# The FFN down projection as seven products per pair of column tiles

## The chip, the core and the metric

The kernel runs on one core of a Trainium2 chip. A core has five engines with a queue each, which run their instructions in order: TensorE (PE: matmuls, with weight loads shown apart as PEld), VectorE (DVE), ScalarE (ACT), GpSimd (POOL) and SyncE (SP, which here only starts DMAs). Matmul results land in PSUM, which has 8 banks of 128 partitions x 512 f32; everything else lives in SBUF. DVE and ACT read PSUM, POOL doesn't. Engines wait for one another by semaphores that a framework sets from what each instruction reads and writes; the order on each engine is the order in which the program emits the instructions (a manual schedule). The metric is device time in microseconds (us), the median of several runs.

## What is computed

One layer of a diffusion backbone for 1024 latent tokens (after 256 context tokens) of width D = 1024: an S5 mixer, a SwiGLU feed-forward network (FFN) of hidden width 2816, and a final norm. The change is in the FFN alone:

```
def swiglu(h, w1, w3, w2):
    return (jax.nn.silu(h @ w1) * (h @ w3)) @ w2
...
x = x + m_l[5][:, None] * swiglu(h_l, ffn_w1[i], ffn_w3[i], ffn_w2[i])
...
return rms_norm(x, norm_final)
```

`h @ w1` and `h @ w3` are the up projection, the product with `w2` the down projection, `m_l[5]` a gate per output channel.

## The kernel before, in words

**The tiles.** The hidden width is cut into NFT = 22 column tiles of 128 ("ft"). For each, the up projection makes 128 x 1024 values g (hidden channel x token), and the down projection multiplies them by 128 rows of `w2` and adds the result to the residual `Y`, which stays in SBUF for all 1024 tokens (8 blocks `s` of 128 tokens, 8 blocks `k` of 128 channels).

**Each product is three matmuls.** An f32 value x is split into hi (x rounded to the narrower matmul type, an ACT cast) and lo (x - hi, a subtraction), and a product is hi·hi + hi·lo + lo·hi (`mm3`, lines 1259 to 1261). `mm4` makes one such product over 512 input channels: 12 matmuls of 128x128 by 128x512. All element-wise work between two tensors goes through the helper `tt` (line 70), so nearly all of it stands on line 70 in the profile and is told apart by the names of its tiles.

**The up projection** of tiles 2 to 21 uses seven products in place of eight (a 2x2 block scheme of Strassen's kind over channel halves, token halves and the two weights): `up` (line 1379) calls `mm(ft, j)` for j = 0 to 6. Their weight operands come from `raw`, four 512-wide pieces of w1 and w3, loaded by `raw13` (SP, line 1172): POOL forms sums and differences (`s5`, `raw[:, 2]`, `raw[:, 0]`, `raw[:, 1]`), and `op_split` puts hi (ACT, line 1201) and lo (POOL) into one of four slots of a ring, `ring`. The moving operands `BV[j]` are made beforehand (`t3_steps`, `t24_steps`, `t1_steps`); `t1_go` finishes the last of them during tile 2. The products' results (`pu`, one PSUM bank each, four banks in turn) are combined by DVE in `t0` to `t3`, with two Silu's on ACT; `gate_up` splits g into hi (ACT, line 1270) and lo (DVE).

**The down projection** (`down`) goes over 8 token blocks and 2 channel halves; each of these 16 makes 3 matmuls into a bank `pd` (four in turn), and DVE adds it to `Y`, 512 elements at a time. `load2` multiplies the 128 x 1024 tile of `w2` by the gate (DVE, 1024 elements) and splits it (ACT line 1002, POOL); `raw2` (SP) loads the next one into the same buffer.

**The order.** After the warm-up tiles 0 and 1, for tile ft = 2 to 19: `load2(ft)`, `up(ft)`, which emits product 0 of ft+1 before its last DVE work, then `down([ft])` with the POOL work of `prep(ft + 1)` between its steps. Tiles 20 and 21 have one `down` in common, in which also the final norm and the stores are made. One tile is 84 + 48 = 132 matmuls.

The kernel before, in the profile's names: `pu` and `pd` are PSUM tiles, `ru`, `rxa`, `rxc`, `r`, `ra`, `c` SBUF regions (`rxc` holds `raw`, `c` the ring, the split g and `w2`, `ru` the residual `Y`, the raw `w2` and `t0`, `t1`; `rxa` holds `t2`, `t3`).

Of the kernel before, what the change touches and what calls it, by code (L numbers as in the profile page):

```python
# [10 lines left out]
F32 = mybir.dt.float32  # L11
R32 = mybir.dt.float32r
I32 = mybir.dt.int32
AF = mybir.ActivationFunctionType
# [3 lines left out]
P = 128  # L18
D = 1024
# [3 lines left out]
NFT = FH // P  # L23
# [14 lines left out]
def s5_ffn_kernel(tc, a, out):  # L38
    nc = tc.nc
    V, S, E, PE, SY = nc.vector, nc.scalar, nc.gpsimd, nc.tensor, nc.sync  # L40
    ctx = ExitStack()
    with ctx:
        ctx.enter_context(tc.manual_schedule())
        sb = ctx.enter_context(tc.tile_pool(name="sb", bufs=1))
        def region(tag, kb, dt=F32):
            return sb.tile([P, int(kb * 256)], dt, tag=tag, name=tag)

        def view(reg, kb, shape, parts=P):
            off = int(round(kb * 256))
# [12 lines left out]
        RXa, RXc = region("rxa", 8), region("rxc", 8)  # L62

        def bc(ap, axis, n):
            sh = list(ap.shape)
# [3 lines left out]
        def tt(o, x, y, op, eng=V):  # L69
            eng.tensor_tensor(out=o, in0=x, in1=y, op=op)  # L70
# [10 lines left out]
        MUL, ADD, SUB = OP.mult, OP.add, OP.subtract  # L81
# [33 lines left out]
        U = view(RU, 0, [G, 160])  # L115
        Y = view(RU, 0, [8, T, P])
# [524 lines left out]
        MB = view(RXa, 0, [2, D])  # L641
# [397 lines left out]
        for i in range(10):  # L1039
# [18 lines left out]
            if i in WSP:  # L1058
                j = 1 - WSP.index(i)
# [111 lines left out]
        def raw13(ft, a0=0, a1=4):  # L1171
            SY.dma_start(wraw[:, 512 * a0:512 * a1], a["w13"][ft].rearrange("p w k n -> p (w k n)")[:, 512 * a0:512 * a1])
# [6 lines left out]
        for cq in range(4):  # L1179
            for s in range(4):  # L1180
                k = 4 * cq + s
# [12 lines left out]
        NPL = 2  # L1194
        CNT = (((0, 0, 0, 0), (2, 2, 2, 0)), ((3, 3, 3, 3), (3, 2, 2, 0)))
        raw = wraw.rearrange("p (a n) -> p a n", a=4)
        ring = [[view(W0, 4 * i + 2 * j, [4, P]) for j in range(2)] for i in range(4)]
        OP_ = {}

        def t_split(o, x, eng):  # L1200
            S.copy(o[0], x)  # L1201
# [44 lines left out]
        def gb(ft):  # L1246
            return GB[ft == NFT - 1]

        def raw2(ft):
            SY.dma_start(w2raw, a["w2"][ft * P:(ft + 1) * P])  # L1250

        def load2(ft):
            tt(w2raw, w2raw, MB[:, 1], MUL)
            split(w2raw, gb(ft)[2:], E)
            if ft + 1 < NFT:
                raw2(ft + 1)

        def mm3(pu, wh, wl, bh, bl, start, stop):
            PE.matmul(pu, wh, bh, start=start, stop=False)  # L1259
# [3 lines left out]
        def mm4(pu, w, b, start, stop):  # L1263
            for k in range(4):
                mm3(pu, w[0][:, k], w[1][:, k], b[0][:, :, k], b[1][:, :, k], start and k == 0, stop and k == 3)

        def gate_up(ft, n, t):
            ns = slice(512 * n, 512 * n + 512)
            gh, gl = gb(ft)[:2]
            S.copy(gh[:, ns], t)  # L1270
            tt(gl[:, ns], t, gh[:, ns].bitcast(F32), SUB)
# [87 lines left out]

        def prep(ft):  # L1360

            if ft > NPL:
                op_split(ft, 1, raw[:, 1])
                yield
# [8 lines left out]
            tt(raw[:, 1], raw[:, 1], raw[:, 0], SUB, E)  # L1373
            yield

        def mm(ft, j):
            pu = pu_()
            mm4(pu, OP_[ft, j], BV[j], True, True)
            return pu

        def up(ft, pu, at={}):

            t0, t1, t2, t3 = tmp
            more = ft + 1 < NFT

            def go(j):
                if j in at:
                    at[j]()

            S.copy(t0, pu)  # L1390
            op_split(ft, 4, raw[:, 3])
            go(0)
            if more:
                raw13(ft + 1, 0, 1)
                raw13(ft + 1, 2, 4)
            tt(t1, mm(ft, 1), t0, ADD)
            S.activation(t1, t1, AF.Silu)
            op_split(ft, 5, raw[:, 1])
            if more:
                raw13(ft + 1, 1, 2)  # L1400
            go(1)
            tt(t0, mm(ft, 2), t0, ADD)
            op_split(ft, 6, s5)
            go(2)
            tt(t2, mm(ft, 3), t0, ADD)
            go(3)
            if more:
                op_split(ft + 1, 0, raw[:, 0])
            pu = mm(ft, 4)
            nx = prep(ft + 1) if ft == NFT - 2 else iter(())  # L1410
            next(nx, None)
            next(nx, None)
            tt(t3, t2, pu, SUB)
            tt(t1, t1, t3, MUL)
            gate_up(ft, 0, t1)
            tt(t0, mm(ft, 5), t0, ADD)
            next(nx, None)
            pu = mm(ft, 6)
            tt(t0, pu, t0, ADD)
            S.activation(t0, t0, AF.Silu)  # L1420
            tt(t2, pu, t2, ADD)
            pu = mm(ft + 1, 0) if more else None
            tt(t0, t0, t2, MUL)
            gate_up(ft, 1, t0)
            for _ in nx:
                pass
            return pu

        def down(fts, last, *others):
            for s in range(T):  # L1430
                for n in range(2):
                    pd = pf([512])
# [44 lines left out]
        h2s(7, tba[1], 0)  # L1477
        h2s(7, tba[1], 1)
        raw2(0)
        rest = iter(())  # L1480
        up_plain(0, 0, rest, {2: lambda: together(h2t_steps(7, pf, tba[1], 0), h2t_steps(7, pf, tba[1], 1)), 3: lambda: mod_row(1, pf)})
        load2(0)
# [13 lines left out]
        NPU[0] = 4  # L1496
        pu = mm(NPL, 0)
        down([NPL - 1], False, prep(NPL))

        def t1_go():  # L1500
            for _ in range(3):
                next(rest, None)

        for ft in range(NPL, NFT - 1):
            load2(ft)
            pu = up(ft, pu, {j: t1_go for j in range(4)} if ft == NPL else {})
            if ft < NFT - 2:
                down([ft], False, prep(ft + 1))
        up(NFT - 1, pu, {2: lambda: load2(NFT - 1)})
# [61 lines left out]
```

## Time and profile before

| | |
|---|---|
| median of 3 runs | 1080.21 us (1078.52 to 1081.13) |
| the profiled execution: span from the first to the last instruction | 1084.0 us |
| mean granted TensorE clock in it | 0.977 |
| instructions | 16631 |
| PE busy, DVE busy, POOL busy, ACT busy | 91%, 70%, 58%, 39% |
| stretch of tiles 2 to 21 | from about 464 us to the end |

For the profiled execution only its span is given; it is 3.8 us above the median of the runs. In the profile a matmul's shown duration overlaps with the next one's, so the rate is read from starts, not from durations. "L70" in front of a row is the helper `tt`; "128x512 f32<-128x512 f32" gives output and input shape, "x" the count, then busy us and mean ns of one. In a timeline, the first number is the start, the second the duration, and in brackets stands how long the engine had been idle and who released it.

### The profile page before, as it was taken

Reading aid. Unit: us, or ns where it says so; the run is one execution under the profiler, and the core shown is the slowest. Engines: PE = TensorE matmul, PEld = TensorE weight load, DVE = VectorE, ACT = ScalarE, POOL = GpSimd, SP = SyncE. Lnnn points to the kernel's source line nnn. Section 1 sums busy time; section 2 is a strip of 40 time slices with the busy share of each in tenths; the row PEclk is TensorE's granted clock in tenths of the full one; section 3 lists DMA queues with packets and bytes.
Section 4 is the critical chain, followed back from the end, with each engine's and each line's share of the span. In section 5 each row is a group of like instructions: output and inputs, shape, how many; then the busy total and the mean of one; then the engine's idle time right before and its main releaser. Section 6 shows DMA issues by size and latency. Waiting matters only on the chain.

```text
span 1084.0 us, 16631 instructions
## 1 busy us (share of the span) xinstructions
PE 990.4 (91%) x6088; PEld 790.4 (73%) x6088; DVE 762.3 (70%) x1783; ACT 418.7 (39%) x833; POOL 631.4 (58%) x501
## 2 busy tenths in 40 slices
PE   4898795656899999999999999999999999999997
PEld 1466521345799997887888888888888888888875
DVE  8979699970665686898766666666766666666657
ACT  4477620453964565423122222222222222222236
POOL 4599666881274364966565555665555555556563
PEclk9998997987999999999999999999999999999999
DMA  8966679675333102110111111111011111111104
GB/s 310 318 124 125 187 231 312 185 142 118 104 114 116 42 2 78 59 38 21 58 59 59 59 59 59 59 59 32 31 56 59 59 59 59 60 59 59 55 23 156
DMA packets 54946, 104.60 MB, mean 96 GB/s; under 512 B 4432, under 2 KB 25168, under 8 KB 53840
## 3 DMA queue, kind: packets, MB, share of 16 engines
q1 hardware_dynamic: 46656, 85.57, 23.7%
q0 software_dynamic: 3888, 14.16, 7.0%
q10 hardware_dynamic: 4320, 3.81, 1.1%
q8 instruction: 48, 0.79, 0.3%
q14 instruction: 34, 0.28, 0.1%
HBM read 83.20 MB, written 6.16 MB: 82 GB/s over the span
## 4 chain that ended last, share of the span: by engine, by line
PE 71%; DMA 9%; POOL 6%; DVE 6%; ACT 5%; issue 2%; SPq 1%; ACTq 0%; DVEq 0%; POOLq 0%
PE pu L1261 11%; PE pu L1260 11%; PE pu L1259 11%; PE pd L1259 7%; PE pd L1260 7%; PE pd L1261 7%; PE pe L1024 3%; PE pe L1025 3%; PE pe L1023 3%; DVE ru L70 2%; POOL c L70 2%; DMA c<-in_ada_w 2%; DMA kd<-r 1%; PE pm L514 1%; DVE rxa L70 1%
## 5 line engine op out<-in xcount | busy, mean ns | idle before, releaser
L70 POOL TENSOR_TENSOR c<-rxc,c 128x512 fp32r<-128x512 f32 x128 | 167.8, 1326 | 185.1 <-ACT c L1201 180.2
L70 DVE TENSOR_TENSOR ru<-pd,ru 128x512 f32<-128x512 f32 x336 | 226.5, 690 | 0.0
L1259 PE MATMUL pu<-ra,c 128*128 128x512 f32 x432 | 168.4, 390 | 0.6 <-ACT ra L1201 0.3
L1261 PE MATMUL pu<-ra,c 128*128 128x512 f32 x432 | 168.4, 390 | 0.6 <-POOL c L70 0.6
L1260 PE MATMUL pu<-ra,c 128*128 128x512 f32 x432 | 168.2, 389 | 0.6 <-DVE ra L70 0.6
L1201 ACT CAST c<-rxc 128x512 fp32r<-128x512 f32 x128 | 76.8, 617 | 188.0 <-POOL rxc L70 107.3
L1259 PE MATMUL pd<-c 128*128 128x512 f32 x336 | 131.0, 390 | 0.7 <-DVE ru L70 0.7
L1260 PE MATMUL pd<-c 128*128 128x512 f32 x336 | 130.7, 389 | 0.0
L1261 PE MATMUL pd<-c 128*128 128x512 f32 x336 | 130.7, 389 | 0.0
L70 DVE TENSOR_TENSOR ru<-pu,ru 128x512 f32<-128x512 f32 x84 | 57.8, 688 | 83.2 <-PE pu L1261 52.4
L70 POOL TENSOR_TENSOR c<-ru,c 128x1024 fp32r<-128x1024 f32 x22 | 53.0, 2407 | 81.7 <-ACT c L1002 73.0
L1261 PEld LDWEIGHTS pu<-ra,c 128*128 128x128 f32 x432 | 81.1, 188 | 18.5 <-POOL c L70 1.7
L1259 PEld LDWEIGHTS pu<-ra,c 128*128 128x128 f32 x432 | 81.1, 188 | 18.1 <-ACT ra L1201 0.8
L1260 PEld LDWEIGHTS pu<-ra,c 128*128 128x128 f32 x432 | 81.1, 188 | 17.7 <-POOL c L70 0.9
L1259 PE MATMUL pu<-c,c 128*128 128x512 f32 x192 | 74.9, 390 | 0.0
L1261 PE MATMUL pu<-c,c 128*128 128x512 f32 x192 | 74.7, 389 | 0.0
L1260 PE MATMUL pu<-c,c 128*128 128x512 f32 x192 | 74.7, 389 | 0.0
L1259 PEld LDWEIGHTS pd<-c 128*128 128x128 f32 x336 | 63.1, 188 | 15.0 <-DVE ru L70 1.9
L1261 PEld LDWEIGHTS pd<-c 128*128 128x128 f32 x336 | 63.1, 188 | 13.2
L1260 PEld LDWEIGHTS pd<-c 128*128 128x128 f32 x336 | 63.1, 188 | 12.9
L70 POOL TENSOR_TENSOR c<-rxc,rxa 128x1024 f32<-128x1024 f32 x30 | 62.0, 2138 | 16.2 <-PE pw L655 10.4
L70 DVE TENSOR_TENSOR ru<-ru,rxa 128x512 f32<-128x512 f32 (+1 forms) x62 | 62.5, 1008 | 7.1 <-ACT ru L1420 3.1
(333 smaller groups left out, 2137.3 us busy)
## 6 DMA issues: line engine op xcount, KB each, us to landing
c<-in_ada_w SPq DMA_DIRECT2D x64, 256.0 KB, 5.4
ru<-in_w SPq DMA_DIRECT2D x22, 512.0 KB, 3.6
c<-c POOLq DMA_DIRECT2D x20, 512.0 KB, 6.7
rxc<-in_w SPq DMA_DIRECT2D x38, 256.0 KB, 4.5
rxc<-in_w SPq DMA_DIRECT2D x19, 512.0 KB, 5.1
ra<-in_ada_w SPq DMA_DIRECT2D x10, 512.0 KB, 11.9
ru<-in_xT SPq DMA_DIRECT2D x4, 1024.0 KB, 8.5
ra<-kd SPq DMA_DIRECT2D x16, 256.0 KB
```

Of the source, the lines that this page charges most:

```text
L70: eng.tensor_tensor(out=o, in0=x, in1=y, op=op)
L514: PE.matmul(pm[32 * b:32 * b + 2], sc3[:, k, 1 - h:3 - h], ada_tile(i), start=i < 4, stop=i >= 60, tile_position=(0, 32 * b))
L1023: PE.matmul(pz, h_[:, k], wH[:, k], start=n == 0, stop=False)
L1024: PE.matmul(pz, h_[:, k], wL[:, k], start=False, stop=False)
L1025: PE.matmul(pz, l_[:, k], wH[:, k], start=False, stop=n == 7)
L1201: S.copy(o[0], x)
L1259: PE.matmul(pu, wh, bh, start=start, stop=False)
L1260: PE.matmul(pu, wh, bl, start=False, stop=False)
L1261: PE.matmul(pu, wl, bh, start=False, stop=stop)
```

## The change

For the nine pairs of tiles (2, 3), (4, 5), ... (18, 19) the down projection of both tiles together is made by a second seven-product scheme, over the two tiles, the two halves of the tokens (s = 0 to 3, 4 to 7) and the two halves of the output channels. A product "D j" is 4 token blocks x 3 matmuls of 512 columns, 12 matmuls, in four PSUM banks. Tiles 0, 1, 20 and 21 keep the old way.

- **Seven products in three PSUM chains.** D1, D7, D6 and D5 add up in the four banks of `XT` (only D1 starts a new sum), D2 and D3 in the four banks of `UT`, D4 alone in `XT`. After each product the running sum is added to (or taken from) one quadrant of `Y` (`d_add(j, h)`, two DVE instructions of 128x1024 per product). For this the quadrant of the second channel half and first token half of `Y` is kept as a difference between `to_diff` (in tile 2) and `from_diff` (in tile 20), four DVE instructions of 1024 elements each.
- **`UT` is shared:** its four banks also take the up products "U j" (bank (j + 3) mod 4), which had a pool of four banks.
- **Operands of g:** DVE forms sums and differences of the four half tiles of g (`rA`, `rB`, `rC`, `t3`) and splits them into four slots `GS` (hi on ACT, lo on DVE).
- **Operands of w2:** two buffers `w2r`, loaded together; the gate is applied by DVE (`gate2`), and POOL forms four sums and differences in place.
- **One ring for all products:** the weights or `w2` operands of all U and D products go through the four slots in the order of `seq`; `produce(i + 4)` is emitted after product i's own work, and its hi cast (ACT) waits until product i, which used the slot, is done.
- **The order in a pair** (f even): U(f,0), then of the pair before D2, D6, D3, D5, then U(f,1), D4, then U(f,2) to U(f,6), D1 of this pair, U(f+1,0), D7, U(f+1,1) to U(f+1,6). That is 21 products, 252 matmuls.
- A region `rw` of 6 KB is added for the second `w2` buffer and `rC`, and the scratch that POOL's own DMAs use for descriptors is set to 8192 bytes.

```diff
-        w2raw = view(RU, 32, [D])
+        w2r = [view(RU, 32, [D]), view(RW, 0, [D])]
...
+        def gate2(ft):
+            tt(w2r[ft % 2], w2r[ft % 2], MB[:, 1], MUL)
...
+        XT = pF.tile([P, 4, 512], F32, tag="x", name="xt")
+        UT = pF.tile([P, 4, 512], F32, tag="u", name="ut")
+
+        RG = [ring[i] for i in range(4)]
+        GS = [[view(G2, 4 * i + 2 * j, [512]) for j in range(2)] for i in range(4)]
...
+        for f in list(PAIRS) + [NFT - 2]:
+            lead = [("U", f, 0), ("D", f - 2, 2), ("D", f - 2, 6), ("D", f - 2, 3), ("D", f - 2, 5), ("U", f, 1), ("D", f - 2, 4)]
+            seq += lead if f > NPL else [("U", f, 0), ("U", f, 1)]
+            seq += [("U", f, j) for j in range(2, 7)]
+            if f in PAIRS:
+                seq += [("D", f, 1), ("U", f + 1, 0), ("D", f, 7)]
+                seq += [("U", f + 1, j) for j in range(1, 7)]
+        seq += [("U", NFT - 1, j) for j in range(7)]
...
+        def produce(i):
...
+            if kind == "D":
+                x = w2_op(j)
+                (b11, b12), (b21, b22) = WB
+                if j == 6:
+                    tt(b12, b22, b11, SUB, E)
+                elif j == 4:
+                    tt(b21, b21, b12, SUB, E)
+                t_split(o, x, E)
+                if j == 1:
+                    tt(b11, b12, b11, SUB, E)
+                    tt(b12, b22, b12, SUB, E)
+                if j == 4:
+                    raw2(ft + 2)
+                    raw2(ft + 3)
+                return
+            x = (raw[:, 0], raw[:, 1], raw[:, 0], raw[:, 2], raw[:, 3], raw[:, 1], s5)[j]
+            t_split(o, x, E)
+            if j == 0:
+                tt(s5, raw[:, 2], raw[:, 3], ADD, E)
+            elif j == 1:
+                tt(raw[:, 2], raw[:, 0], raw[:, 2], SUB, E)
+                tt(raw[:, 0], s5, raw[:, 0], SUB, E)
+            elif j == 3:
+                tt(raw[:, 1], raw[:, 1], raw[:, 0], SUB, E)
...
+        def d_mm(i):
...
+            gh, gl = GS[{1: 0, 7: 1, 2: 0, 6: 1, 3: 2, 5: 3, 4: 0}[j]]
+            bank = UT if j in (2, 3) else XT
+            for s in range(4):
+                cs_ = slice(s * P, s * P + P)
+                for n, (w, b) in enumerate(((gh, wh), (gh, wl), (gl, wh))):
+                    PE.matmul(bank[:, s], w[:, cs_], b, start=j in (1, 2, 4) and n == 0, stop=n == 2,
+                              skip_group_check=j not in (1, 2, 4))
...
+            y = Y[:, k0:k0 + 4, s0 + 2 * h:s0 + 2 * h + 2].rearrange("p k s n -> p s k n")
+            tt(y, y, bank[:, 2 * h:2 * h + 2].rearrange("p s (k n) -> p s k n", k=4), op)
...
+            else:
+                tt(t0, pu, t0, ADD)
+                S.activation(t0, t0, AF.Silu)
+                tt(t2, pu, t2, ADD)
...
+                elif f:
+                    tt(rB, t0, t2, MUL)
+                    tt(rA, rA, rB, SUB)
+                else:
+                    tt(t3, t0, t2, MUL)
+                    tt(rA, t3, rA, SUB)
...
+        def after_u0(ft):
+
+            if NPL <= ft - 1 < NFT - 2 and ft % 2 == 0:
+                hi(GS[1], rA)
+                tt(rC, rA, rC, SUB)
+                lo(GS[1], rA)
+                hi(GS[2], rC)
+
+        def post_d(j):
+
+            if j == 1:
+                hi(GS[1], rA)
+                d_add(1, 0)
+                lo(GS[1], rA)
+                d_add(1, 1)
+            elif j == 2:
+                d_add(2, 0)
+                lo(GS[2], rC)
+                d_add(2, 1)
+                tt(rB, rB, t3, ADD)
+                hi(GS[3], rB)
+            elif j == 6:
+                d_add(6, 0)
+                lo(GS[3], rB)
+                d_add(6, 1)
+            elif j == 3:
+                hi(GS[0], t3)
+                d_add(3, 0)
+                d_add(3, 1)
+                lo(GS[0], t3)
+            else:
+                d_add(j, 0)
+                d_add(j, 1)
...
+        for i, (kind, ft, j) in enumerate(seq):
+            if i:
+                (u_mm if kind == "U" else d_mm)(i)
+            if kind == "D":
+                post_d(j)
+            else:
+                post_u(ft, j)
+                if j == 0:
+                    after_u0(ft)
+            if kind == "U" and ft in PAIRS and j in (2, 3):
+                gate2(ft + j - 2)
+            produce(i + 4)
+            if kind == "U":
+                if ft == NPL and j < 4:
+                    t1_go()
+                if ft == NPL and j == 5:
+                    to_diff()
+                if ft == NFT - 2 and j in (2, 3):
+                    from_diff(j - 2)
```

More of the change, by code (lines that the diff above doesn't have):

```diff
@@ L1373, in prep, with pd_ @@
             tt(raw[:, 1], raw[:, 1], raw[:, 0], SUB, E)
+            raw13(ft + 1, 0, 1)
             yield
[L1376 to L1427, printed above, removed]
+        def pd_(i):
+            return XT[:, i % 4] if XT is not None else pf([512])
+        XT = None
         def down(fts, last, *others):
@@ L1479, in s5_ffn_kernel @@
         raw2(0)
+        raw2(1)
         rest = iter(())
@@ L1495, in s5_ffn_kernel @@
         pF = psF.__enter__()
-        NPU[0] = 4
-        pu = mm(NPL, 0)
-        down([NPL - 1], False, prep(NPL))
+        XT = pF.tile([P, 4, 512], F32, tag="x", name="xt")
+        UT = pF.tile([P, 4, 512], F32, tag="u", name="ut")
+        RG = [ring[i] for i in range(4)]
+        GS = [[view(G2, 4 * i + 2 * j, [512]) for j in range(2)] for i in range(4)]
+        rA, rB, rC = R0[:, 0:512], R0[:, 1036:1548], view(RW, 4, [512])
+        t0, t1, t2, t3 = tmp
+        WB = [[w[:, 512 * n:512 * n + 512] for n in range(2)] for w in w2r]
@@ new lines, in w2_op @@
+        def w2_op(i):
+            (b11, b12), (b21, b22) = WB
+            return {1: b11, 7: b12, 2: b21, 6: b12, 3: b22, 5: b11, 4: b21}[i]
+        PAIRS = range(NPL, NFT - 2, 2)
+        seq = []
+        for f in list(PAIRS) + [NFT - 2]:
[5 more added lines that the diff above has]
+                seq += [("U", f + 1, j) for j in range(1, 7)]
@@ new lines, in s5_ffn_kernel, with cut @@
+        seq += [("U", NFT - 1, j) for j in range(7)]
+        def cut(o, x):
+            t_split(o, x, V)
+        def produce(i):
+            if i >= len(seq):
+                return
+            kind, ft, j = seq[i]
+            o = [t.rearrange("p k n -> p (k n)") for t in RG[i % 4]]
+            if kind == "D":
+                x = w2_op(j)
+                (b11, b12), (b21, b22) = WB
+                if j == 6:
[9 more added lines that the diff above has]
+                    raw2(ft + 3)
+                return
+            x = (raw[:, 0], raw[:, 1], raw[:, 0], raw[:, 2], raw[:, 3], raw[:, 1], s5)[j]
[7 more added lines that the diff above has]
+                tt(raw[:, 1], raw[:, 1], raw[:, 0], SUB, E)
+                if ft + 1 < NFT:
+                    raw13(ft + 1, 0, 1)
+            elif j == 4 and ft + 1 < NFT:
+                raw13(ft + 1, 2, 4)
+            elif j == 5 and ft + 1 < NFT:
+                raw13(ft + 1, 1, 2)
@@ new lines, in u_bank, with u_mm @@
+        def u_bank(j):
+            return UT[:, (j + 3) % 4]
+        def u_mm(i):
+            kind, ft, j = seq[i]
+            mm4(u_bank(j), RG[i % 4], BV[j], True, True)
+        def d_mm(i):
+            kind, ft, j = seq[i]
+            wh, wl = (t.rearrange("p k n -> p (k n)") for t in RG[i % 4])
+            gh, gl = GS[{1: 0, 7: 1, 2: 0, 6: 1, 3: 2, 5: 3, 4: 0}[j]]
[5 more added lines that the diff above has]
+                              skip_group_check=j not in (1, 2, 4))
@@ new lines, in to_diff, with from_diff, hi, lo @@
+        def to_diff():
+            for h in range(2):
+                tt(quad(4, 0, h), quad(4, 0, h), quad(4, 4, h), SUB)
+                tt(quad(4, 0, h), quad(4, 0, h), quad(0, 0, h), SUB)
+        def from_diff(h):
+            tt(quad(4, 0, h), quad(4, 0, h), quad(4, 4, h), ADD)
+            tt(quad(4, 0, h), quad(4, 0, h), quad(0, 0, h), ADD)
+        def hi(o, x):
+            S.copy(o[0], x)
+        def lo(o, x, eng=V):
+            tt(o[1], x, o[0].bitcast(F32), SUB, eng)
+        def post_u(ft, j):
+            pu, plain, f = u_bank(j), ft >= NFT - 2, ft % 2 == 0
+            if j == 0:
+                S.copy(t0, pu)
+            elif j == 1:
+                tt(t1, pu, t0, ADD)
+                S.activation(t1, t1, AF.Silu)
+            elif j == 2:
+                tt(t0, pu, t0, ADD)
+            elif j == 3:
+                tt(t2, pu, t0, ADD)
+            elif j == 4:
+                tt(t3, t2, pu, SUB)
+                if plain:
+                    tt(t1, t1, t3, MUL)
+                    gate_up(ft, 0, t1)
+                else:
+                    r = rA if f else rC
+                    tt(r, t1, t3, MUL)
+                    cut(GS[0], r)
+            elif j == 5:
+                tt(t0, pu, t0, ADD)
+            else:
+                tt(t0, pu, t0, ADD)
+                S.activation(t0, t0, AF.Silu)
+                tt(t2, pu, t2, ADD)
+                if plain:
+                    tt(t0, t0, t2, MUL)
+                    gate_up(ft, 1, t0)
+                elif f:
[4 more added lines that the diff above has]
+                    tt(rA, t3, rA, SUB)
@@ L1502, in t1_go @@
                 next(rest, None)
[L1504 to L1509, printed above, removed]
+        u_mm(0)
+        down([NPL - 1], False, prep(NPL))
+        raw2(NPL)
+        raw2(NPL + 1)
+        for i, (kind, ft, j) in enumerate(seq):
[3 more added lines that the diff above has]
+                post_d(j)
+            else:
+                post_u(ft, j)
+                if j == 0:
+                    after_u0(ft)
[9 more added lines that the diff above has]
+                    from_diff(j - 2)
+                if ft == NFT - 2 and j == 3:
+                    load2(NFT - 2)
+                if ft == NFT - 1 and j == 2:
+                    load2(NFT - 1)
         SY.dma_start(NFb.rearrange("p k n -> p (k n)"), a["norm_final"].to_broadcast([P, D]))
```

24 lines of the change are left out of this document (14 added, 10 removed).

## The prediction, made before the changed kernel ran

> **What bounds the kernel now.** I read the page's busy shares first, then a table of windows over the loop, then the timelines of the engines.
>
> ```profile
> span 1084.0 us, 16631 instructions
> PE 990.4 (91%) x6088; PEld 790.4 (73%) x6088; DVE 762.3 (70%) x1783; ACT 418.7 (39%) x833; POOL 631.4 (58%) x501
> ```
>
> ```profile
> 455.00:492.00 37.00, 36.20 (x158) 29.31 (x157) 33.31 (x40) 11.87 (x21) 26.27 (x18) 1.00 0.13 44
> 500.00:1020.00 520.00, 520.00 (x2294) 430.27 (x2294) 346.91 (x494) 135.61 (x224) 288.13 (x211) 1.00 0.16 52
> ```
>
> The columns are window, length, then PE, PEld, DVE, ACT and POOL busy. From 500 to 1020 us PE is never idle: 2294 matmuls in 520 us, one every 0.2267 us at full clock (1.00). A tile of 132 matmuls takes 29.9 us, a pair 59.8, and DVE (67%), POOL (55%) and ACT (26%) fit beside it. So before, a matmul less is worth 0.2267 us, and nothing else in the loop costs anything. Only the stretch of tiles 1 and 2 (455 to 492) is different: DVE is busy 33.31 of 37 us, and PE has lost 0.8.
>
> **What goes.** A pair had 264 matmuls and gets 252. Nine pairs save 9 x 12 x 0.2267 = **24.5 us** while PE stays the bound. The 21 products of a pair, 12 x 0.2267 = 2.72 us each, then take 57.1 us.
>
> **Do the other engines still fit?** In sums, yes. Prices:
>
> ```profile
> L70 DVE TENSOR_TENSOR ru<-pd,ru 128x512 f32<-128x512 f32 x288 | 195.1, 691 | 0.0
> L70 DVE TENSOR_TENSOR ru<-ru,rxa 128x1024 f32<-128x1024 f32 x18 | 21.9, 1216 | 0.0
> ```
>
> A pair's 32 additions of 0.69 become 14 of 1024 elements. Such an addition out of PSUM isn't in the trace; its bounds are this 1.22 and twice 0.69 = 1.38. I take 1.22: one operand in PSUM changed nothing at 512 elements. DVE then has 14 x 1.22 + 2 x 1.22 (gates) + 14 x 0.69 (up products) + 14 x 0.69 (seven splits, seven products and differences of g) = 39 us of 57. POOL has 21 lo's, 8 sums for the up and 4 for the down: 33 x 1.3 = 43 us. But sums don't decide: D products come in a chain, and all queues are in order. I therefore walk the order of emission. The steps between instructions:
>
> ```profile
> 610.23 0.69 DVE L70 TENSOR_TENSOR rxa<-rxa,pu 128x512 f32<-128x512 f32 x1 [2.03 <-PE pu L1261]
> 611.02 0.69 DVE L70 TENSOR_TENSOR ru<-ru,rxa 128x512 f32<-128x512 f32 x1
> 612.40 0.69 DVE L70 TENSOR_TENSOR c<-ru,c 128x512 fp32r<-128x512 f32 x1 [0.69 <-ACT c L1270]
> 613.01 0.68 DVE L70 TENSOR_TENSOR ru<-pu,ru 128x512 f32<-128x512 f32 x1
> ...
> 616.39 0.63 ACT L1420 ACTIVATE ru<-ru 128x512 f32<-128x512 f32 x1 [4.03 <-DVE ru L70]
> 617.06 0.69 DVE L70 TENSOR_TENSOR ru<-ru,rxa 128x512 f32<-128x512 f32 x1
> 617.78 0.62 ACT L1270 CAST c<-ru 128x512 fp32r<-128x512 f32 x1 [0.76 <-DVE ru L70]
> 618.31 0.62 ACT L1201 CAST c<-rxc 128x512 fp32r<-128x512 f32 x1
> 619.00 1.30 POOL L70 TENSOR_TENSOR c<-rxc,c 128x512 fp32r<-128x512 f32 x1 [7.93 <-ACT c L1201]
> 620.26 1.29 POOL L70 TENSOR_TENSOR r<-rxc 128x512 f32<-128x512 f32 x1
> 621.63 1.30 POOL L70 TENSOR_TENSOR rxc<-rxc 128x512 f32<-128x512 f32 x1
> ...
> 813.80 0.39 PE L1261 MATMUL pu<-ra,c 128*128 128x512 f32 x1
> 814.23 0.69 DVE L70 TENSOR_TENSOR ru<-pu,ru 128x512 f32<-128x512 f32 x1 [1.27 <-PE pu L1261]
> ```
>
> On DVE an instruction that needs the last one's result starts 0.79 after it (610.23 to 611.02), one that doesn't 0.61 (612.40 to 613.01), 0.08 before its end; so I pace a 1.22 at 1.14. ACT casts follow at 0.53, POOL at 1.26 or, dependent, 1.37. ACT to DVE takes 0.04 (616.39 + 0.63 to 617.06), DVE to ACT the same within 0.01 (617.75 to 617.78), ACT to POOL 0.07; DVE starts 0.20 after the last matmul's slot (813.80 + 0.23).
>
> **The lead of a pair.** Set 0 at the end of U(f-1,6), f even. PE has six products until D4: U(f,0), D2, D6, D3, D5, U(f,1), 16.3 us. Beside them runs one chain. *DVE and ACT:* t0 at 0.20, Silu 0.93, t0·t2 1.60, rA 2.39, rC 3.18, lo(GS1) 3.79 (its hi cast ends at 3.74), the first half of D2's addition 4.40, lo(GS2) 5.54, the second half 6.15, rB + t3 7.29, done 7.98. *ACT and POOL:* hi(GS3) 8.02 stands in ACT's queue before the hi cast for U(f,1), so that goes at 8.55. On POOL follow lo of U(f,1) 9.24, raw2 10.50, raw0 11.87, and only then b21 - b12 for D4, 13.13, done 14.43. *Back:* the hi cast for D4 has waited at the head of ACT's queue and goes at 14.5, hi(GS0) behind it at 15.0, done 15.6. DVE stands at lo(GS0), 15.7, and the addition of D5 is queued behind it: first half 16.3 to 17.5. D4 starts a new sum in the banks that this addition reads, so PE gets on at 17.7, with 0.05 and a slow first matmul:
>
> ```profile
> 1044.06 2.29 POOL c L70
> 1046.35 0.04 issue
> 1046.40 0.50 PE pu L1261
> ```
>
> Bare, the chain is 1.4 us longer than PE's six products. Now the port:
>
> ```profile
> 1032.01 1.29 POOL L70 TENSOR_TENSOR c<-rxc,c 128x512 fp32r<-128x512 f32 x1 [1.87 <-ACT c L1201]
> 1032.48 1.36 DVE L70 TENSOR_TENSOR c<-ru,c 128x512 fp32r<-128x512 f32 x1 [1.79 <-ACT c L1270]
> 1033.26 1.74 POOL L70 TENSOR_TENSOR r<-rxc 128x512 f32<-128x512 f32 x1
> ```
>
> A DVE instruction with both inputs in SBUF, begun inside POOL's, ends 0.54 after POOL's end (1033.30 to 1033.84) instead of 0.69 after its own start, and POOL's next is stretched from 1.3 to 1.74. With a PSUM input there is no such stretch (691 above). Mean costs:
>
> ```profile
> L70 DVE TENSOR_TENSOR ru<-ru,rxa 128x512 f32<-128x512 f32 x34 | 29.3, 862 | 3.5
> L70 DVE TENSOR_TENSOR c<-ru,c 128x512 fp32r<-128x512 f32 x35 | 24.6, 702 | 24.0 <-ACT c L1270 24.0
> ```
>
> ```profile
> L70 DVE TENSOR_TENSOR rxa<-ra,c 128x512 f32<-128x512 f32 x4 | 5.4, 1362 | 0.0
> L70 DVE TENSOR_TENSOR rxa<-rxa,ra 128x512 f32<-128x512 f32 x4 | 4.2, 1053 | 0.0
> L70 DVE TENSOR_TENSOR rxa<-rxa,c 128x512 f32<-128x512 f32 x4 | 3.7, 934 | 0.1
> L70 DVE TENSOR_TENSOR c<-ru,c 128x512 fp32r<-128x512 f32 x2 | 2.8, 1380 | 1.4 <-ACT c L1270 1.4
> L70 DVE TENSOR_TENSOR ra<-rxa,ra 128x512 fp32r<-128x512 f32 x2 | 2.5, 1241 | 2.1 <-ACT ra L1201 2.1
> ```
>
> In the loop (500 to 1020, POOL busy 55%) the wait is 0.78 - 0.69 = 0.09 on average; from 455 to 492 (POOL 71%) the 16 take 18.6 us, so 0.47 each. In the changed loop POOL is busy 43 of some 62 us, 69%, nearer to the second, so I take 0.4 for the seven such DVE steps of the chain. Its four POOL steps can each lose 0.44 like the one above; DVE's seven hold the port 4.8 of 21 us, so I take a third of that, 0.15: together 2.8 + 0.6. The chain is 21.1 us, PE loses **4.8 per lead, 43.2 in nine** (ends: 0.09 and 0 give 18.3, so 2.0 and 18; 0.47 and 0.44 give 22.8, so 6.5 and 58). Nothing covers it: the operands' ring is four products deep and its next casts stand in the same ACT queue.
>
> **D7.** After U(f,6), rB stands at 1.60, rA 2.39, D1's additions and lo(GS1) behind: 3.00, 4.14, 4.75. D7 starts at 5.44; three waits of 0.4 make it about 0.5 late, **4** in eight pairs (0 to 7).
>
> **Tile 2.** The finishing of `BV[6]` already fills DVE:
>
> ```profile
> 477.44 0.69 DVE L70 TENSOR_TENSOR ru<-pd,ru 128x512 f32<-128x512 f32 x1
> ...
> 498.37 0.69 DVE L70 TENSOR_TENSOR ru<-ru,rxa 128x512 f32<-128x512 f32 x1
> ```
>
> The last addition of tile 1 is at 477.44, t0·t2 of tile 2 at 498.37. Before that come now a second gate and four `to_diff`'s, 5 x (1.14 + 0.47) = 8.05, then rA 0.79 and D1's first half (0.61 until it starts, 1.22): 509.0. PE could be at D7 at 477.24 + 8 x 2.72 = 499.0. That is 10 us, of which about 1 was lost before: **+9** (6 to 14).
>
> **Tiles 20 and 21.** Four `from_diff`'s stand in DVE's queue where 14 U products follow one another without a D; I take **+3** (0 to 5). The last `down` is as before.
>
> **The scratch** for POOL's DMAs concerns the mixer:
>
> ```profile
> c<-c POOLq DMA_DIRECT2D x20, 512.0 KB, 6.7
> ```
>
> 20 such transfers, and 7 like them out of `rxc`; at least 0, at most 27 x 6.7 = 181 us if each held POOL for a landing. I take 0, the nearest row giving no wait of POOL's own, and leave the other end to the tail.
>
> **Sum** against the profiled span: 1084.0 - 24.5 + 43.2 + 4 + 9 + 3 = 1118.7. The median of the runs is 3.8 below that span, so 1114.9; I say **1115**.
>
> **Rivals.** *The port is free when it matters.* With waits of zero a lead costs 1.4, D7 nothing, tile 2 about 7 (5 x 0.47 less), the tail 0: -24.5 + 12.6 + 7 = -5, **1075**; if rB + t3 or POOL's three steps also come 1.4 earlier, PE stays the bound and 1063 is left. It decides from a chain under 16.3 us. For it: the loop's 0.09. Against: the 0.47 where both engines are full. *The clock drops.* Rows for it:
>
> ```profile
> 244.00:248.00 4.00, 0.12 (x1) 0.16 (x1) 0.00 (x0) 0.00 (x0) 2.24 (x2) 0.50 0.57 125
> 248.00:252.00 4.00, 4.00 (x18) 3.56 (x20) 0.00 (x0) 0.00 (x0) 0.65 (x1) 0.52 0.96 183
> ```
>
> After a long idle stretch the next 4 us, PE full again, run at 0.52 (the granted clock is the third number from the right). At D4 PE would stand for some 4 us at a time; if each stop leaves 4 us at half clock, nine leads lose 2 more each: **1133**. Against it: full clock wherever gaps are short, as from 455 to 492. The Trainium skill (TensorE: Matmul & The Clock Gate, Part 1: The HAM clock gate) says that the clock is halved after one idle window of about 3.4 us, and that these windows run freely; by that a stop of 4 us would rarely hold a whole one. The two rows agree with the halving; whether 4 us suffice no run here shows. *The four-bank tiles are waited for as a whole.* Then every U waits for the DVE step of the U before it, 0.20 + 0.69 + 0.15 = 1.0, some 140 times: about **1250**. I see no four-bank tile in the rows; SBUF regions are waited for by part.
>
> **Chances.** Forecast 0.68 (1095 to 1130); port free 0.14 (1060 to 1085, of which 0.03 within 0.3% of 1080.2 and 0.11 faster by more); clock 0.12; whole tiles or the scratch 0.06. 0.3%, about 3 us, is what a measurement of this kernel can tell from no change. Faster 0.11, same 0.03, slower 0.86. The range leaves out the quicker part of the second case and the last: **1080 to 1137**.
>
> **What would show it.** Right: PE idle before D4 about 4 us nine times, released by DVE's addition of D5; ACT's cast for D4 waiting for POOL; DVE's two-SBUF rows at 1.0 to 1.1 us; a pair of 62 us. Wrong: pairs of 57 to 58 us with PE full (port free), granted clock under 1 in the loop (clock), stops before each U (whole tiles), or a later start of the loop (scratch).

## The result, and the profile after

The changed kernel takes **1315.59 us** (median of 4 runs, 1310.0 to 1320.93) beside 1080.16 us for the kernel before: a ratio of 1.2175 (95% interval 1.2134 to 1.2216). It is slower by 235 us, where 35 were forecast, and outside the range.

The first lines of the changed kernel's page, and two groups of its matmuls (busy time and mean ns of one, then the idle time of PE just before them and what ended it):

```profile
span 1319.0 us, 16655 instructions
PE 1052.0 (80%) x5980; PEld 782.3 (59%) x5980; DVE 803.6 (61%) x1692; ACT 453.2 (34%) x905; POOL 735.5 (56%) x582
...
L1261 PE MATMUL ut<-ra,c 128*128 128x512 f32 x400 | 165.5, 414 | 84.0 <-DVE ru L71 44.7
L1531 PE MATMUL xt<-c,c 128*128 128x512 f32 x540 | 142.9, 417 | 43.1 <-DVE ru L71 43.1
```

The 108 matmuls are gone (6088 before), but PE fell from 91% to 80% of a longer span, and no other engine is fuller than 61%. PE waits, and it waits for DVE, ahead of up products (`ut`) and down products (`xt`) alike. The waits of PE, summed (total, times, longest):

```profile
PE ut L1261 <- DVE ru L71: 44.7, 51, 1.3
PE xt L1531 <- DVE ru L71: 43.1, 27, 3.0
PE ut L1261 <- DVE rxa L71: 39.4, 40, 3.0
PE xt L1261 <- DVE ru L71: 25.6, 30, 2.8
PE ut L1261 <- ACT ru L1586: 16.6, 11, 1.8
```

These five sum to 169.4 us. PE's timeline shows how it looks in a stretch without down products, where one up product follows another (first matmuls of successive products):

```profile
699.55 0.50 PE L1261 MATMUL ut<-ra,c 128*128 128x512 f32 x1 [0.85 <-DVE ru L71]
...
703.44 0.47 PE L1261 MATMUL ut<-ra,c 128*128 128x512 f32 x1 [0.88 <-DVE ru L71]
...
707.28 0.47 PE L1261 MATMUL ut<-ra,c 128*128 128x512 f32 x1 [0.88 <-DVE rxa L71]
```

A product starts every 3.84 to 3.89 us instead of every 2.72. Each stands until DVE has read the product before it, although that one lies in another bank. So four banks that were meant to be used in turn work like one. Of the 1.12 us lost per product 0.88 shows as idle; the rest, 0.24, is the last matmul's full 0.39 us in place of the 0.23 from one start to the next, and a slower first one. The other side of the same thing, on the down products: D7 on PE, and its two additions on DVE.

```profile
692.99 2.98 PE L1531 MATMUL xt<-c,c 128*128 128x512 f32 x12 [1.39 <-DVE ru L71]
```

```profile
691.64 1.21 DVE L71 TENSOR_TENSOR ru<-ru,xt 128x1024 f32<-128x1024 f32 x1
696.01 2.35 DVE L71 TENSOR_TENSOR ru<-ru,xt 128x1024 f32<-128x1024 f32 x2 [3.17 <-PE xt L1531]
```

D7 starts 0.14 us after the end (692.85) of D1's *second* half addition, and D7's first half addition, which needs 6 of its 12 matmuls, starts only when all 12 are through (692.99 + 2.98 = 695.97).

### The profile page after: what moved, and what is told of

Same layout as the page of the kernel before. It is cut to its first block, busy times and chain, and to the rows that moved or that the text cites. A ratio compares the mean times of both kernels' runs of the same rounds, so it can differ in the third digit from the quotient of the medians.

```text
span 1319.0 us, 16655 instructions
## 1 busy us (share of the span) xinstructions
PE 1052.0 (80%) x5980; PEld 782.3 (59%) x5980; DVE 803.6 (61%) x1692; ACT 453.2 (34%) x905; POOL 735.5 (56%) x582
## 3 DMA queue, kind: packets, MB, share of 16 engines
q1 hardware_dynamic: 46656, 85.57, 19.3%
## 4 chain that ended last, share of the span: by engine, by line
PE 50%; DVE 27%; POOL 7%; ACT 6%; DMA 4%; issue 4%; SPq 1%; ACTq 0%; DVEq 0%; POOLq 0%
DVE ru L71 12%; PE ut L1261 10%; PE ut L1263 8%; PE ut L1262 8%; PE xt L1531 5%; DVE ra L71 3%; DVE rxa L71 3%; POOL c L71 2%; PE pe L1025 2%; POOL rxc L71 2%; PE pe L1026 2%; PE pe L1024 2%; DVE r L71 2%; PE ut L1531 2%; DVE c L71 2%
## 5 line engine op out<-in xcount | busy, mean ns | idle before, releaser
L1261 PE MATMUL ut<-ra,c 128*128 128x512 f32 x400 | 165.5, 414 | 84.0 <-DVE ru L71 44.7
L1531 PE MATMUL xt<-c,c 128*128 128x512 f32 x540 | 142.9, 417 | 43.1 <-DVE ru L71 43.1
L1262 PE MATMUL ut<-ra,c 128*128 128x512 f32 x400 | 158.0, 395 | 0.0
L1263 PE MATMUL ut<-ra,c 128*128 128x512 f32 x400 | 157.6, 394 | 0.0
L1261 PEld LDWEIGHTS ut<-ra,c 128*128 128x128 f32 x400 | 76.5, 191 | 133.6 <-ACT c L1202 60.7
L1531 PEld LDWEIGHTS xt<-c,c 128*128 128x128 f32 x540 | 105.7, 200 | 75.9 <-issue 53.8
L71 DVE TENSOR_TENSOR ru<-ru,xt 128x1024 f32<-128x1024 f32 x90 | 107.0, 1213 | 61.9 <-PE xt L1531 61.9
L71 DVE TENSOR_TENSOR ru<-ut,ru 128x512 f32<-128x512 f32 x80 | 55.2, 690 | 120.9 <-PE ut L1263 120.9
L71 POOL TENSOR_TENSOR c<-ru,c 128x512 fp32r<-128x512 f32 (+1 forms) x39 | 54.7, 1403 | 78.2 <-ACT c L1202 60.6
L1263 PEld LDWEIGHTS ut<-ra,c 128*128 128x128 f32 x400 | 76.2, 191 | 16.9
L1262 PEld LDWEIGHTS ut<-ra,c 128*128 128x128 f32 x400 | 76.3, 191 | 13.4
L1261 PE MATMUL ut<-c,c 128*128 128x512 f32 x160 | 64.4, 402 | 17.3 <-ACT ru L1586 16.6
L1263 PE MATMUL ut<-c,c 128*128 128x512 f32 x160 | 63.3, 396 | 0.0
L1262 PE MATMUL ut<-c,c 128*128 128x512 f32 x160 | 63.1, 395 | 0.0
L1531 PE MATMUL ut<-c,c 128*128 128x512 f32 x216 | 54.2, 399 | 9.9 <-ACT ru L1565 6.1
L71 POOL TENSOR_TENSOR rxc<-rxc 128x512 f32<-128x512 f32 x40 | 55.9, 1399 | 0.1
L1531 PEld LDWEIGHTS ut<-c,c 128*128 128x128 f32 x216 | 39.1, 188 | 24.9 <-ACT ru L1565 9.9
```

The source lines that it names most:

```text
L1262: PE.matmul(pu, wh, bl, start=False, stop=False)
L1263: PE.matmul(pu, wl, bh, start=False, stop=stop)
L1531: PE.matmul(bank[:, s], w[:, cs_], b, start=j in (1, 2, 4) and n == 0, stop=n == 2, skip_group_check=j not in (1, 2, 4))
```

## The experiments

**Theory:** the four banks of `UT`, and those of `XT`, are declared as one tile each, and a tile of several banks is waited for as a whole: a matmul into any bank waits for every reader of the tile, a reader of any bank for every matmul into it. **Rival:** the waits are the real dependences of the lead's chain that the prediction walked, only longer (DVE slowed by POOL). The first four runs split or join tiles, with the bank numbers and the size of the additions that go with it, and change nothing else.

**Two tiles of two banks each** for `XT` and `UT`, successive up products going to different tiles:

```diff
-        XT = pF.tile([P, 4, 512], F32, tag="x", name="xt")
-        UT = pF.tile([P, 4, 512], F32, tag="u", name="ut")
+        XT = [pF.tile([P, 2, 512], F32, tag=f"x{h}", name="xt") for h in range(2)]
+        UT = [pF.tile([P, 2, 512], F32, tag=f"u{h}", name="ut") for h in range(2)]
...
```

> The changed kernel with XT and UT each cut into two PSUM tiles of two banks; consecutive U products and consecutive steps of down go to different tiles; nothing else. Theory A (a read of a PSUM tile is waited for as a whole tile, so in the changed kernel every product waits for the reading of the product before it, though that is another bank): these stops go, and what is left is the chain of the lead as the prediction walked it: 1115 us, 1095 to 1135. Rival B (the time is lost in the D products' running sums or in the two-SBUF port, and the tiles don't matter): it stays above 1280.

Measured: 1129.39 us, ratio to the kernel before 1.0434 (1.0398 to 1.0470). 186 us go with two declarations and the bank order that belongs to them. A D7 shows the other side too: it runs from 697.17 to 700.48, and its first half addition now starts 1.56 us before its end.

```profile
697.17 3.31 PE L1532 MATMUL xt<-c,c 128*128 128x512 f32 x12 [0.30 <-DVE ru L71]
```

```profile
698.92 1.22 DVE L71 TENSOR_TENSOR ru<-ru,xt 128x1024 f32<-128x1024 f32 x1 [0.17 <-PE xt L1532]
700.51 1.22 DVE L71 TENSOR_TENSOR ru<-ru,xt 128x1024 f32<-128x1024 f32 x1 [0.37 <-PE xt L1532]
```

**Eight tiles of one bank**, the additions as four of 512 elements instead of two of 1024:

```diff
+        XT = [pF.tile([P, 512], F32, tag=f"x{h}", name="xt") for h in range(4)]
+        UT = [pF.tile([P, 512], F32, tag=f"u{h}", name="ut") for h in range(4)]
...
+            for s in (2 * h, 2 * h + 1):
+                y = Y[:, k0:k0 + 4, s0 + s]
+                tt(y, y, bank[s].rearrange("p (k n) -> p k n", k=4), op)
```

> XT and UT as eight PSUM tiles of one bank; each addition to Y of 128x1024 becomes two of 128x512, so DVE has 28 x 0.69 = 19.3 us in place of 14 x 1.22 = 17.1 us in a pair. Theory A: 1100 to 1140, within 1.5% of the run with two-bank tiles (no product or down step is held at all, but DVE's chain in the lead gets 3 x 0.08 longer). Rival B: above 1280.

Measured: 1125.16 us, ratio 1.0377 (1.0338 to 1.0416). PE's waits for a DVE that reads another bank are gone; the largest waits left in the loop:

```profile
PE xt L1531 <- DVE ru L71: 26.8, 9, 3.0
PE xt L1531 <- DVE c L71: 6.0, 18, 0.4
PE xt L1531 <- ACT c L1557: 5.4, 1, 5.4
```

**Only `XT` split** into two tiles of two banks, `UT` left as it was:

> The changed kernel with only XT cut into two tiles of two banks; UT, which the up products use, stays one tile of four banks. Theory A: the stops of the two down loops and of D1, D7, D6, D5, D4 go, those of the 140 U products and of D2 and D3 stay: 1115 + 120 x 1.1 = about 1250 (1225 to 1275). Rival B: above 1280. If nearly all is won here (under 1150), the U products were not what cost.

Measured: 1247.38 us, ratio 1.1517 (1.1465 to 1.1568). The waits of the up products are the changed kernel's to within a microsecond, and the two `down` loops lost theirs (25.6 to 1.6):

```profile
PE ut L1261 <- DVE ru L71: 45.6, 51, 1.9
PE ut L1261 <- DVE rxa L71: 39.4, 40, 3.1
...
PE xt L1261 <- DVE ru L71: 1.6, 2, 1.4
```

**The kernel before, with its `pu` banks of tiles 2 to 21 as one tile of four banks:**

```diff
-            return pF.tile([P, 512], F32, tag="u", name="pu", bufs=NPU[0])
...
+            if not UT4:
+                UT4.append(pF.tile([P, 4, 512], F32, tag="u", name="pu"))
+            UT4.append(0)
+            return UT4[0][:, len(UT4) % 4]
```

> The kernel before, with the four banks of the up products of tiles 2 to 21 declared as one tile of four banks instead of four tiles; nothing else. Theory A: each of some 130 products waits for the step that reads the one before it, 3.84 us a product in place of 2.72 as in the changed kernel: 1080 + 130 x 1.1 = about 1225 (1190 to 1250). Rival B: 1080, no change.

Measured: 1324.75 us, ratio 1.2231 (1.2177 to 1.2285). The direction was right, the size was missed by 100 us, because ACT reads these banks too:

```profile
PE pu L1265 <- ACT ru L1396: 67.8, 20, 3.6
PE pu L1265 <- DVE ru L70: 51.8, 62, 1.2
PE pu L1265 <- DVE rxa L70: 35.8, 40, 1.8
PE pu L1265 <- ACT ru L1426: 28.0, 19, 1.5
```

The DVE part (102 stops for 87.6 us) is close to the price per stop that was expected. On top, ACT's copy of U0's bank (line 1396) stands in ACT's queue behind the `w2` cast, and now U1 has to wait for that copy. The last row names a Silu that reads no bank; DVE's second reading of U6's bank ends within 0.1 us of it (801.30 and 801.37 in one tile), so this row too goes back to a reader of the tile. None of the down projection's seven-product scheme is in this kernel, and it is as slow as the changed one, though in part by other readers: the declaration alone is enough to cost that much. The first theory holds, the rival doesn't explain 190 of the 235 us. What in the framework makes it wait by tile no run shows; the PSUM pools of both kernels are opened with one setting throughout (`reuse_waits="tile"`).

**What is left: 41 us.** Here the prediction's own chain can be read, in one lead of the kernel with one-bank tiles. POOL's difference for D4, ACT's casts for D4 and (behind it) of D3's operand, DVE's rest of that operand with D5's additions behind it, and D4 on PE:

```profile
731.29 1.30 POOL L71 TENSOR_TENSOR rw<-rw,ru 128x512 f32<-128x512 f32 x1
```

```profile
732.62 0.62 ACT L1202 CAST c<-rw 128x512 fp32r<-128x512 f32 x1 [5.68 <-POOL rw L71]
733.15 0.61 ACT L1557 CAST c<-rxa 128x512 fp32r<-128x512 f32 x1
```

```profile
733.79 1.34 DVE L71 TENSOR_TENSOR c<-rxa,c 128x512 fp32r<-128x512 f32 x1 [2.65 <-ACT c L1557]
735.06 2.46 DVE L71 TENSOR_TENSOR ru<-ru,xt 128x512 f32<-128x512 f32 x4
```

```profile
735.88 4.34 PE L1531 MATMUL xt<-c,c 128*128 128x512 f32 x12 [2.98 <-DVE ru L71]
```

DVE is idle for 2.65 us in the middle of "its" backlog, and ACT for 5.68: each only waits for the next. If that is so, moving one POOL instruction is enough.

**The difference for D4 earlier:** behind the rest of D6's operand instead of ahead of D4's.

```diff
-                elif j == 4:
-                    tt(b21, b21, b12, SUB, E)
                 t_split(o, x, E)
+                if j == 6:
+                    tt(b21, b21, b12, SUB, E)
```

> One-bank tiles with one POOL instruction moved: the difference of two w2 blocks for D4 is issued behind D6's rounding-rest instead of ahead of D4's own. Theory A (the stop before D4 is a queue chain: POOL's difference late, ACT's cast for D4 waits 5.68 us for it, ACT's cast of D3's operand stands behind that cast, DVE's rest of that operand waits 2.65 us for ACT, D5's additions stand behind it on DVE, and D4 needs the banks they read): the nine stops of 2.98 us go, 26.8 us, and with them the clock that fell to 0.65 behind each, 1.2 to 1.6 us each; against them a stop of some 0.7 to 1.1 us ahead of D6 or D5 comes up. From 1125: 1085 to 1100 us, clock of the run up by 0.01. Theory B (the stop is DVE's backlog itself, additions that last 1.67 us instead of 0.69 while POOL holds the port): the work of DVE and POOL is the same, so D4 stops as long, and the time stays within 5 us of 1125.

Measured: 1094.88 us, ratio 1.0114 (1.0077 to 1.0150): 30 us less, theory A. The nine stops at D4 are gone, and the short ones ahead of products whose operand DVE has still to cut went from 6.0 to 12.2 us:

```profile
PE xt L1531 <- DVE c L71: 12.2, 27, 0.6
```

The loop's window (length, then PE, PEld, DVE, ACT, POOL busy, then granted clock), with one-bank tiles and with the difference early as well:

```profile
520.00:1040.00 520.00, 490.76 (x2076) 396.23 (x2076) 367.28 (x486) 162.44 (x281) 374.16 (x270) 0.97 0.16 49
```

```profile
520.00:1040.00 520.00, 508.13 (x2193) 407.90 (x2192) 396.21 (x516) 169.99 (x293) 399.13 (x284) 1.00 0.17 53
```

2193 matmuls instead of 2076 pass in the same 520 us, and the granted clock is back at 1.00.

**The sum rB + t3 on POOL as well** (`tt(rB, rB, t3, ADD, E)`):

> As the run with the early difference, and the sum of the two product columns (rB + t3, behind D2) on POOL instead of DVE: DVE loses ten instructions of 1.0 to 1.3 us in the leads, POOL gains ten of 1.3 us. Theory A (DVE's order in the lead is what is left): 0.5 us of each lead goes, some 5 us less than the run with the early difference, 1080 to 1095. Theory B (the port is what is left): POOL's 1.30 us holds DVE off just as long, within 2 us of it or slower.

Measured: 1088.83 us, ratio 1.0086 (1.0055 to 1.0117). The medians differ by the expected size, but the intervals of the two runs overlap, so this one stays undecided.

**Without the difference quadrant** (one-bank tiles, no `to_diff` and `from_diff`, so that this quadrant of the result is not the reference's):

> One-bank tiles without the four subtractions behind column tile 2's U5 and the four additions in column tile 20 that keep one quadrant of the residual as a difference (left out, so that quadrant's sums are not the reference's): prices the terms of the first and the last pair. DVE loses eight instructions of 1.2 us each. If they lie on the path as the prediction put them (part of +9 in tile 2 and +3 in tiles 20 and 21): 6 to 9 us less than 1125. If they lie beside other work: within 2 us of 1125.

Measured: 1113.49 us, ratio 1.0297 (1.0252 to 1.0343): 12 us less, more than either theory expected. The loops of the two profiles, from U1 of tile 2 to the end, differ by more, 652.9 against 633.6 us: the stages ahead of the loop, which this edit doesn't touch, vary between executions, and U1 starts at 471.6 in one and at 477.5 in the other. Of these 19.3 us, 8.3 lie ahead of the first D4: D7's stop of 5.4 us in tile 2 and the slow clock behind it. 5.3 lie behind the start of the last D4, 2.5 of them stops in tile 20. The third part, 5.7 over the eight pairs between, came unasked. Four D4's of this profile, each after a like stop:

```profile
604.39 3.00 PE L1531 MATMUL xt<-c,c 128*128 128x512 f32 x12 [2.98 <-DVE ru L71]
666.08 3.00 PE L1531 MATMUL xt<-c,c 128*128 128x512 f32 x12 [2.96 <-DVE ru L71]
...
791.04 4.43 PE L1531 MATMUL xt<-c,c 128*128 128x512 f32 x12 [2.93 <-DVE ru L71]
854.17 4.24 PE L1531 MATMUL xt<-c,c 128*128 128x512 f32 x12 [2.93 <-DVE ru L71]
```

The same stop leaves D4's 12 matmuls at full speed in the first two pairs (61.69 us from one to the next) and slow in the two later ones (63.13 us); the granted clock over them is 1.00 and 1.00, then 0.65 and 0.67. So a lost clock costs some 1.4 us per stop, and whether it is lost isn't set by the stop's length. In the kernel with one-bank tiles all nine D4's are slow (4.31 to 5.46 us; the one shown above takes 4.34), here six: three clocks that held, 1.3 to 2.5 us each, are the third part.

**The lead in another order:** U0, U1, D2, D6, D3, D5, U2, D4, with the difference early, the sum on POOL and the up products one bank earlier.

> As the run with early difference and sum on POOL, with the lead of a pair in another order: U0, U1, D2, D6, D3, D5, U2, D4 instead of U0, D2, D6, D3, D5, U1, D4, and the U products one bank earlier in the ring. Theory A (what is left in a lead is the cut of the D operands, which ACT, DVE and POOL must make between the end of U0 and the products that read it): one product more ahead of D2 covers it, the stops ahead of D6 and D5 go, 0.8 us of each pair is gained, and the pair lasts 58.5 us: 1072 to 1090 us, level with the kernel before (1080 to 1084) at best, since the stops of column tile 2 stay. Theory B (DVE's total of work in a pair is the bound): no gain over the run without the new order, or slower.

Measured: 1079.88 us, ratio 0.9983 (0.9965 to 1.0001). Level with the kernel before: theory A. PE's waits for DVE's rest of a down operand, 8.2 us in the run before, are down to 0.3; a new stop of 0.35 us at D2 has come up in each lead, and a pair lasts 58.1 us.

**And D7 one product later,** behind U(f+1,1):

```diff
-                seq += [("D", f, 1), ("U", f + 1, 0), ("D", f, 7)]
+                seq += [("D", f, 1), ("U", f + 1, 0), ("U", f + 1, 1), ("D", f, 7)]
```

> As the run with the reordered lead, and the second product of a first half, D7, behind U1 of the odd column tile instead of behind its U0. In the run before it D7 waits 7.0 us for ACT's cast of its operand in column tile 2, and one more product of 2.72 us ahead of it covers that much of the wait; in the other pairs the short stop ahead of D7's second half goes. Theory A (the stops of column tile 2 are DVE's backlog of additions and differences, which the longer cover shortens): 2 to 3 us less in column tile 2, up to 0.5 us less in each of the other eight pairs, so 1071 to 1078 us, faster than the kernel before by 0.3 to 1 per cent. Theory B (moving D7 back only moves the stop to the U product behind it, because the rounding-rest for U2 is late on POOL): within 2 us of 1080.

Measured: **1074.28 us, ratio 0.9926 (0.9906 to 0.9946)**: theory A, and faster than both kernels, than the one before by 0.7%. D7's stop in tile 2 shrank from 7.0 to 3.6 us, and the loop is nearly full:

```profile
PE xt L1531 <- ACT c L1557: 3.6, 1, 3.6
```

```profile
520.00:1000.00 480.00, 476.87 (x2093) 392.12 (x2093) 368.82 (x483) 162.44 (x287) 400.27 (x283) 1.00 0.17 54
```

## Why the prediction was wrong, point by point

**The step that failed** is the sentence that put the whole-tile case aside: "I see no four-bank tile in the rows; SBUF regions are waited for by part." It carried banks over from the kernel before, where each bank is a tile of its own, to a declaration in the diff that makes four banks one tile. The terms before it leaned on the same reading: "in the banks that this addition reads" (the banks, not the tile), up products priced at 2.72 us, the last `down` "as before". The runs showed the whole-tile wait in its place: 186 of the 235 us go when the two tiles are cut in two, 190 when they are cut in four. That no four-bank row stood there was no evidence: in these stages no tile of the kernel before had more than one bank, so none of their rows could show it, and the case deserved a large chance. Elsewhere the same trace does hold a tile of two banks, `pv` in the mixer, and it shows the wait. Eight transposes fill it, four to a bank, and line 537 on ACT copies the first bank alone:

```profile
36.76 0.60 PE L433 MATMUL pv<-r,c 128*128 128x128 f32 x4
...
36.76 1.04 PE L433 MATMUL pv<-r,c 128*128 128x128 f32 x8
...
37.84 0.58 ACT L537 COPY c<-pv 128x512 f32<-128x512 f32 x1 [0.71 <-PE pv L433]
```

The first bank is filled at 37.36 (the first four), the second at 37.80; ACT, idle for 0.71 us, starts at 37.84.

**The rival's own price** was half of it. "1.0 us some 140 times" is near for the up products: 51 + 40 + 11 waits for 100.7 us, and with `XT` split the cut of `UT` is worth 118 us (1247.38 to 1129.39). It left out `XT`, whose cut is worth 68 us (1315.59 to 1247.38): the down products' waits beyond those of the lead, and the two old `down` loops, which go through `XT` (25.6 us and their clock, below). That is why it said 1250 and not 1316.

**The rest, against the kernel with one-bank tiles.** Its span is 40.5 us longer than the kernel before's, but in that execution the stages ahead of the loop were 5.6 us shorter. From U1 of tile 2 to the end it is 652.9 us (from 471.6) against 606.8 (from 477.2), so the terms have to make +46.1:

| term | predicted | measured, and from what |
|---|---|---|
| 108 matmuls | -24.5 | 5980 instead of 6088 |
| nine leads, stops | +43.2 | 26.8 idle, 2.98 each |
| nine leads, clock | 0 (a rival: 2 each) | 14.6: nine D4's of 4.31 to 5.46 us instead of 3.00 |
| D7 and other late operands | +4 | 6.0 in 18 stops |
| drain and slow first matmul at each stop | 0, but for one in the lead | about 9, some 0.3 at each of 29 stops |
| tile 2 | +9 | about 10: 7.1 idle ahead of D1 and D7 (1.74 and 5.40), then D1's last ten matmuls in 4.14 us and D7's twelve in 5.57 instead of 2.56 and 2.9, less the 1 lost before |
| tiles 20, 21 | +3 | 2.4: 2.9 idle with `from_diff` (0.4 without), 0.5 in the kernel before |
| sum | +34.7 | some 45 of 46 |

So the 1115 lies near the 1125 of this kernel partly by luck: the leads' stops were put 16 us too high, and the clock and the restarts, together some 24, were left out.

- *The chain of the lead* was right link by link: POOL's difference, ACT's cast, DVE's rest, D5's additions, D4, nine times. The stop was put at 4.8 us and is 2.98, with two short stops of at most 0.4 us elsewhere in the pair, 0.27 at D5 and 0.41 at D7.
- *The port* was right in size: in the loop of that kernel the ten groups of DVE instructions of 512 elements with both inputs in SBUF take 0.68 to 1.67 us, 1.04 on average over 127, where 1.0 to 1.1 was forecast. Four of the groups:

```profile
L71 DVE TENSOR_TENSOR c<-r,c 128x512 fp32r<-128x512 f32 x33 | 25.2, 764 | 5.5 <-ACT c L1202 5.5
L71 DVE TENSOR_TENSOR r<-ru,rxa 128x512 f32<-128x512 f32 x16 | 22.1, 1380 | 2.0 <-DVE rxa L71 0.5
...
L71 DVE TENSOR_TENSOR c<-rw,c 128x512 fp32r<-128x512 f32 x18 | 18.2, 1010 | 6.2 <-ACT c L1202 6.2
L71 DVE TENSOR_TENSOR r<-rxa,r 128x512 f32<-128x512 f32 x9 | 15.0, 1666 | 0.3
```

- *The clock rival and the forecast both held in part.* They were given as alternatives, but a stop and what the clock does behind it add up: a pair lasts 61.7 us where the clock holds (62 was forecast) and 63.1 where it doesn't.
- *The scratch* costs nothing that can be seen. In the kernels with the smaller scratch and one-bank tiles the sixteen additions of tile 1 end between 472.5 and 479.2 us, and before the last of them ended at 478.1. With one-bank tiles alone:

```profile
461.62 10.87 DVE L71 TENSOR_TENSOR ru<-xt,ru 128x512 f32<-128x512 f32 x16
```

- *Port free* was wrong as it stood. That the last run takes 1074 where it said 1075 is a coincidence of numbers: the port was not free there (DVE's groups with both inputs in SBUF still take up to 1.67 us), but the chain was cut, the lead reordered and D7 moved.

## What to carry to other kernels

Read the declarations in a diff as closely as the instructions: how a buffer is cut into tiles decides what is waited for, and a rotation through banks of one tile is no rotation. A case that no row of a stage can show isn't made unlikely by that; another stage may have the row, as the mixer has here. When a stop stays, follow it back through idle engines to the one instruction that is late; here one POOL subtraction, issued four products earlier, was worth 30 us.

## What the runs showed of the hardware

**Short gaps take the clock down.** With `XT` as one tile, the old `down` loop of tile 1 does 3 matmuls, waits 0.78 us for DVE, and so on. First matmuls of its steps in the changed kernel, and the granted clock (the third number from the right) in two windows of it:

```profile
466.84 0.50 PE L1261 MATMUL xt<-c 128*128 128x512 f32 x1 [0.78 <-DVE ru L71]
...
468.59 0.58 PE L1261 MATMUL xt<-c 128*128 128x512 f32 x1 [0.78 <-DVE ru L71]
...
473.24 0.80 PE L1261 MATMUL xt<-c 128*128 128x512 f32 x1 [0.79 <-DVE ru L71]
...
475.67 0.80 PE L1261 MATMUL xt<-c 128*128 128x512 f32 x1 [0.78 <-DVE ru L71]
```

```profile
467.00:472.00 5.00, 3.43 (x9) 1.78 (x9) 1.38 (x2) 2.14 (x4) 4.19 (x5) 0.69 0.00 0
482.00:487.00 5.00, 3.34 (x7) 1.66 (x6) 1.38 (x2) 0.00 (x0) 0.00 (x0) 0.50 0.00 0
```

The step grows from 1.75 to 2.43 us, and the clock stays at 0.50 as long as the gaps go on. Gaps of 0.88 us in steps of 3.84, among the up products, do not do it: this window of the changed kernel holds the loop.

```profile
560.00:1260.00 700.00, 558.96 (x2247) 420.43 (x2248) 389.47 (x405) 175.48 (x304) 394.89 (x292) 0.98 0.12 40
```

So the length of one gap alone doesn't decide. The idle share differs (0.78 of 1.75, against 0.88 of 3.84), and with it the busy stretch between gaps; no run separates these two. The Trainium skill (TensorE: Matmul & The Clock Gate, A second HAM failure mode: psum-queue depth-cycling) tells of PE pausing so often between groups of matmuls that the clock swings; the trace agrees that short pauses can halve it, but here it stays at 0.50 and doesn't swing.

**One stop under 3 us can do it too.** The Trainium skill, on the same page (TensorE: Matmul & The Clock Gate, Part 1: The HAM clock gate), lets the clock be halved after one idle window of about 3.4 us; here stops of 2.93 to 2.98 us did it in some pairs and not in others, so the measurement goes below that figure. Stops of 2.3 us ahead of D4 did it as well: with two-bank tiles three of nine D4's run at a granted clock of 0.62 to 0.66, and with only `XT` split seven of nine at 0.60 to 0.63, the others at 1.00. That equal stops end differently fits the windows that run freely by this part of the Trainium skill; their phase no run here shows.
